# Loading each attention head's tiles half a head ahead, and parking three heads' outputs in DRAM

## The chip, the cores and the metric

The kernel runs on one core of one Trainium2 chip. The metric is the device time of one execution in microseconds (us). TensorE (PE) does the matrix products, VectorE (DVE), ScalarE (ACT) and GpSimd (POOL) the element-wise work, and SyncE (SP) issues nearly all transfers (DMAs) between DRAM and the on-chip memory SBUF; products are summed up in PSUM. SP issues its DMAs in the order of its program, and an issue that must wait holds all that stand behind it.

## The reference, cut to what matters

One layer on x of 1024 rows by 1024 columns in float32: half a feed-forward block, a mixer with two branches of attention, half a second feed-forward block, and a norm. The change lies in the mixer alone.

```
u = rms_norm(x, mix_norm)
q_a, k_a, v_a, q_b, k_b, v_b, gate_logits = split(u @ w_mix_in)
y_a = chunked_band_attention(q_a, k_a, v_a, rel_bias_a)     # branch A: 8 heads of 64
y_b = diff_attention(q_b, k_b, v_b, t5_bias, lam, subln_g)  # branch B: 4 heads of 128
g_a, g_b = split(sigmoid(gate_logits + b_gate))
merged = g_a * (y_a @ w_branch_a) + g_b * (y_b @ w_branch_b)
x = x + merged @ w_o
```

In branch A a chunk of 64 rows attends to itself and to the 8 chunks before it. In branch B each head has two score matrices; with a bias b the softmax of the second, times lam, is taken from the softmax of the first, and the difference is multiplied by v:

```
sc = einsum('bqhrd,bkhrd->bhrqk', qblk, k) * scale + bias   # r = 0, 1; keys up to the query's chunk
p = softmax(sc)
attn = p[:, :, 0] - lam * p[:, :, 1]
o = rms_norm(attn @ v, subln_g) * (1 - lambda_init)
```

## The kernel before, in words

All values of matrix products are kept as two parts, a rounded high part and the low rest, and a product takes three matmuls (high x high, high x low, low x high; `mm3`, lines L128 to L130).

The stage that changes lies between the mixer's projections, which write q, k, v and the gates g to DRAM, and the output projection. It has eight heads in a row: A0 to A3 (each of them two heads of branch A side by side) and B0 to B3. For a head `load_qkv` fetches four tiles of 1 MB: qs, ks, kl (k with its two parts swapped) and vt. They come from a pool `big` of 14 buffers of 1 MB, which also holds the bias tiles nb and the outputs y of the heads (1 MB each, high and low part of 1024 rows). A new tile takes the buffer of one that is done with; a load into it has to wait until the last reader of that one is through. nb is made by `bias_rows` with eight small DMAs from a table in DRAM; each A head has its own, B0 and B1 share one, B2 and B3 another. The outputs y of all eight heads stay in SBUF until they are multiplied by w_branch_a or w_branch_b.

Every head is cut into eight jobs. A job is a Python generator with five steps: scores (`sc`, L779, L780), bias and softmax (DVE at L787, ACT at L789); nothing; transposes of the probabilities (`pt`, L795); the product with vt (`pv`, L943, L944 in branch B); and in branch B the norm and a matmul that turns and scales the result (`try`, L958), whose split into high and low part is y (DVE at L104). `run` takes up a new job in each round and carries the four before it one step on, so that five jobs overlap, over the edges of heads as well. A head's first job issues the head's loads, in its own first step.

Beside the jobs of branch B runs a filler, `branch_a`: 16 steps, one for every two jobs of B. A step loads a gate tile gl (128 x 512), makes y_a @ w_branch_a for it (`pb`, 12 matmuls), multiplies by gl on DVE (L892) and stores the result ta (L893). `pb` takes a PSUM buffer of the tag "pv", which has two. After the stage the same is done with y_b and w_branch_b, where the gate and ta are loaded, and the results merged.

Each engine's order is settled when the kernel is built: a scheduler takes the instructions of all this and puts them in the order in which, by its own model of costs, they get ready. So a program text that issues a load earlier also moves other instructions against each other.

## Time and profile before

| | us |
|---|---|
| three runs of the kernel before | 2159.69, 2159.53, 2156.72 (median 2159.53) |
| the profiled execution, its own time | 2157.48 |
| its span in the trace | 2155.1 |
| PE busy | 2074.9 (96%) |
| DVE busy | 1460.8 (68%) |
| ACT busy | 975.0 (45%) |
| POOL busy | 193.3 (9%) |

The attention stage takes from about 1060 to 1355 us of the span; head B0's first scores stand at about 1175 and those of B3, the last head, at about 1293. In a profile's row the first column is the start in us, the second the time busy; x8 at its end says that eight like it stand together, and [1.41 <-DMA kl<-kx] that the engine stood idle for 1.41 us before, until that DMA had landed. "PEclk" is the granted clock of TensorE as a share of the higher of its two levels, 2.4 GHz.

### The profile page before, as it was taken

What the parts mean: (1) busy time and instruction counts of PE and PEld (TensorE: products, weight loads), DVE (VectorE), ACT (ScalarE), POOL (GpSimd) and SP (SyncE); (2) the same over time, 40 slices, a digit from 0 to 9 for tenths busy, and PEclk for the clock granted to TensorE, in tenths of its full rate; (3) what the DMA queues carried; (4) which work ended last, traced back from release to release, by engine and by line L of the source; (5) the groups of instructions that cost most, each with busy time, mean ns of one, the idle gap of its engine ahead of it and who ended that gap; (6) DMA issues with size and microseconds to landing.
All of it is one profiled execution on the core that took longest, in us unless ns stands there. A gap on an engine that the chain in (4) does not pass through costs nothing.

```text
span 2155.1 us, 29016 instructions
## 1 busy us (share of the span) xinstructions
PE 2074.9 (96%) x10025; PEld 1730.3 (80%) x10025; DVE 1460.8 (68%) x2678; ACT 975.0 (45%) x1911; POOL 193.3 (9%) x290
## 2 busy tenths in 40 slices
PE   6999999999999999999999988898999999999997
PEld 5788888888888788899788877776788888888886
DVE  7666566577577756566488877777766656658566
ACT  5433333334446544444498665135433333334444
POOL 2120000000001000000066233201000000000001
PEclk9999999999999999999999999999999999999999
DMA  6653333294345544553682365614643333366344
GB/s 193 174 169 111 96 95 118 93 336 133 118 130 158 169 143 164 195 196 137 224 279 103 134 210 184 230 59 157 181 156 92 114 94 96 114 244 220 98 118 156
DMA packets 277572, 333.55 MB, mean 155 GB/s; under 512 B 15421, under 2 KB 168013, under 8 KB 277425
## 3 DMA queue, kind: packets, MB, share of 16 engines
q1 hardware_dynamic: 276096, 327.94, 46.8%
q0 software_dynamic: 1184, 3.24, 0.6%
q8 instruction: 79, 1.29, 0.3%
q14 instruction: 69, 0.56, 0.1%
q10 hardware_dynamic: 144, 0.52, 0.1%
HBM read 226.45 MB, written 105.19 MB: 154 GB/s over the span
## 4 chain that ended last, share of the span: by engine, by line
PE 80%; DVE 7%; DMA 5%; ACT 4%; issue 3%; SPq 1%; POOL 0%; ACTq 0%; DVEq 0%; POOLq 0%
PE prod L128 19%; PE prod L129 19%; PE prod L130 18%; PE po L129 6%; PE po L130 6%; PE po L128 6%; DVE wlo L102 2%; ACT whi L97 1%; ACT pm L789 1%; PE tr L205 1%; PE pb L128 1%; PE pb L130 1%; PE pb L129 1%; PE pt L795 1%; PE sc L779 1%
## 5 line engine op out<-in xcount | busy, mean ns | idle before, releaser
L129 PE MATMUL po<-wlo,whi 128*128 128x512 f32 x728 | 285.2, 392 | 5.5 <-DVE wlo L102 5.4
L130 PE MATMUL po<-whi,wlo 128*128 128x512 f32 x728 | 283.9, 390 | 0.0
L97 ACT CAST whi<-raw 128x512 fp32r<-128x512 f32 x200 | 124.4, 622 | 311.5 <-PE prod L129 244.4
L97 ACT CAST whi<-T 128x512 fp32r<-128x512 f32 x196 | 121.9, 622 | 249.7 <-PE prod L129 228.5
L97 ACT CAST whi<-B 128x512 fp32r<-128x512 f32 x178 | 110.8, 623 | 266.1 <-PE po L129 258.2
L113 DVE TENSOR_TENSOR c<-prod,c 128x512 f32<-128x512 f32 x190 | 131.1, 690 | 133.3 <-PE prod L130 122.3
L102 DVE TENSOR_TENSOR wlo<-raw,whi 128x512 fp32r<-128x512 f32 x200 | 138.6, 693 | 106.2 <-ACT whi L97 64.8
L102 DVE TENSOR_TENSOR wlo<-B,whi 128x512 fp32r<-128x512 f32 x178 | 122.4, 688 | 127.3 <-ACT whi L97 127.3
L128 PE MATMUL po<-whi 128*128 128x512 f32 x728 | 198.8, 391 | 0.4 <-DVE xc L507 0.3
L102 DVE TENSOR_TENSOR wlo<-T,whi 128x512 fp32r<-128x512 f32 x196 | 134.6, 687 | 92.5 <-ACT whi L97 91.6
L139 POOL TENSOR_TENSOR r<-v,neg_half 128x1 f32<-128x1 f32 x64 | 50.3, 790 | 1324.2 <-DVE v L180 1225.9
L129 PEld LDWEIGHTS po<-wlo,whi 128*128 128x128 f32 x728 | 136.9, 188 | 38.0 <-DVE wlo L102 9.8
L128 PEld LDWEIGHTS po<-whi 128*128 128x128 f32 x728 | 136.7, 189 | 29.9 <-ACT whi L97 1.4
L130 PEld LDWEIGHTS po<-whi,wlo 128*128 128x128 f32 x728 | 136.9, 188 | 28.2
L102 DVE TENSOR_TENSOR wlo<-N,whi 128x512 fp32r<-128x512 f32 x64 | 44.1, 689 | 113.2 <-PE prod L129 62.9
L102 DVE TENSOR_TENSOR wlo<-ha,whi 128x512 fp32r<-128x512 f32 x154 | 105.4, 684 | 9.0 <-ACT whi L97 9.0
L272 ACT COPY c<-prod 128x512 f32<-128x512 f32 x186 | 103.1, 586 | 11.2 <-DMA hA<-c 4.3
L97 ACT CAST whi<-ha 128x512 fp32r<-128x512 f32 x154 | 94.8, 615 | 16.9 <-PE prod L129 11.4
L789 ACT ACTIVATE pm<-pm,mn 128x640 f32<-128x640 f32 (+7 forms) x128 | 94.0, 736 | 11.9 <-DVE ri L924 6.3
L128 PE MATMUL prod<-A11h,whi 128*128 128x512 f32 x240 | 95.7, 399 | 2.6 <-ACT A11h L97 2.6
L128 PE MATMUL prod<-S1h,whi 128*128 128x512 f32 x240 | 94.1, 392 | 3.1 <-ACT S1h L97 2.1
L787 DVE CUSTOM_DVE_ANT_0 pm<-sc,nb 128x640 f32<-128x640 f32 (+7 forms) x128 | 87.9, 698 | 12.5 <-PE sc L780 5.9
(246 smaller groups left out, 5369.4 us busy)
## 6 DMA issues: line engine op xcount, KB each, us to landing
raw<-in_ffn_w_in_dram SPq DMA_DIRECT2D x98, 512.0 KB, 4.4
raw<-in_w_mix_in_dram SPq DMA_DIRECT2D x47, 512.0 KB, 4.5
ha<-hS SPq DMA_DIRECT2D x88, 256.0 KB, 2.7
hA<-c SPq DMA_DIRECT2D x66, 256.0 KB, 4.3
ha<-hA SPq DMA_DIRECT2D x66, 256.0 KB, 2.7
B<-in_ffn_w_out_dram SPq DMA_DIRECT2D x12, 1024.0 KB, 10.3
hS<-hs SPq DMA_DIRECT2D x44, 256.0 KB, 3.0
hS<-c SPq DMA_DIRECT2D x44, 256.0 KB, 4.5
```

The source lines that it names most:

```text
L97: nc.scalar.copy(out=hi, in_=src)
L102: (nc.gpsimd if on_pool else nc.vector).tensor_tensor(out=lo, in0=src, in1=h, op=ALU.subtract)
L113: nc.vector.tensor_tensor(out=out_, in0=a, in1=b, op=op)
L128: nc.tensor.matmul(ps, a[0], b[0], start=first, stop=False, skip_group_check=shared)
L129: nc.tensor.matmul(ps, a[0], b[1], start=False, stop=False, skip_group_check=shared)
L130: nc.tensor.matmul(ps, a[1], b[0], start=False, stop=last, skip_group_check=shared)
L139: nc.gpsimd.tensor_tensor(out=r, in0=v, in1=neg_half, op=ALU.pow)
L205: nc.tensor.transpose(tr[:, k, :], rows[:, k * P:(k + 1) * P], ident)
L272: nc.scalar.copy(out=self.held[name], in_=p)
L779: nc.tensor.matmul(sc[:, m, :wc], qs[:, h, c], ks[:, h, kc], start=True, stop=False)
L787: nc.vector.tensor_tensor_reduce(out=d3, in0=sc, in1=nb.rearrange("p (n w) -> p n w", n=n), scale=1.0, scalar=3e38, op0=ALU.add, op1=ALU.m ...
L789: nc.scalar.activation(out=dst, in_=dst, func=AF.Exp, bias=mn, scale=-1.0, accum_out=rs)
```

## The change

A head's loads and its nb move from its first job into a function `begin`, which is put into the list of jobs by itself, behind the fourth job of the head before; `run` calls it there. The first head begins at once, and its qs, ks and kl are loaded in two halves (`load_qkv(pr, 2)`). y is still allocated in the first job. The last job of B0, B1 and B2 now stores the head's y to a new DRAM tensor `y_d`; behind the sixth job of B3 three calls of `load_y` take new tiles from the pool and load them back, and they, with B3's y from SBUF, are what the stage behind multiplies by w_branch_b.

```diff
@@ -572,6 +572,7 @@
     v_d = drams(2, [S, 2 * HALF], "v", F32R)
     g_d = drams(2 * KT, [P, S], "g")
     ta_d = drams(KT, [P, S], "ta")
+    y_d = drams(3, [P, 2, S], "y", F32R)
     diag_a = dram.tile([A_HEADS, SKEW, EA], F32, name="diag_a")
     diag_b = dram.tile([B_HEADS, SKEW, EB], F32, name="diag_b")
     rows = lambda a: [a[t * P:(t + 1) * P, :] for t in range(NT)]
@@ -746,7 +747,7 @@
         flush()
 
 
-    ys = []
+    ys, last_y = [], []
     with tc.tile_pool(name="ps2", bufs=1, space=PSUM) as ps:
         e1, e2 = (small.tile([P, 1], F32, tag="le", bufs=2, name="le") for _ in range(2))
         nc.scalar.activation(out=e1, in_=lams[0], func=AF.Exp)
@@ -808,9 +809,12 @@
 
 
 
-        def run(jobs, filler=None):
+        def run(jobs):
             live = []
-            for step, job in enumerate(list(jobs) + [None] * 4):
+            for job in list(jobs) + [None] * 4:
+                if callable(job):
+                    job()
+                    continue
                 for g in [job] + live[::-1] if job else live[::-1]:
                     next(g, None)
                 live = (live + [job] if job else live)[-4:]
@@ -819,14 +823,16 @@
         def jobs_a(pr):
             ctx_ = {}
 
+            def begin():
+                ctx_["qkv"] = load_qkv(pr, 1 if pr else 2)
+                ctx_["nb"] = big([P, 2, S], "nb", F32)
+                for hh in range(2):
+                    bias_rows(ctx_["nb"][:, hh, :WA], diag_a, 2 * pr + hh, EA, WA)
+
             def job(sb_, h):
-                if not ctx_:
-                    ctx_["qkv"] = load_qkv(pr)
+                if "y" not in ctx_:
                     ctx_["y"] = big([P, 2, S], "y")
                     ys.append(ctx_["y"])
-                    ctx_["nb"] = big([P, 2, S], "nb", F32)
-                    for hh in range(2):
-                        bias_rows(ctx_["nb"][:, hh, :WA], diag_a, 2 * pr + hh, EA, WA)
                 qkv, y, nb = (ctx_[n] for n in ("qkv", "y", "nb"))
                 vt = qkv[3]
                 i0, i1 = 2 * sb_, 2 * sb_ + 1
@@ -875,7 +881,7 @@
                 if h == 1:
                     c = slice(sb_ * 256, (sb_ + 1) * 256)
                     split(ysum, y[:, 0, c], y[:, 1, c], on_pool=True)
-            return [job(sb_, h) for sb_ in range(4) for h in range(2)]
+            return begin, [job(sb_, h) for sb_ in range(4) for h in range(2)]
 
 
         def branch_a():
@@ -897,16 +903,19 @@
         def jobs_b(hb, filler):
             ctx_ = {}
 
+            def begin():
+                ctx_["qkv"] = load_qkv(4 + hb)
+                if hb % 2 == 0:
+                    nbs.append(big([P, 2, S], "nb", F32))
+                    for hh in range(2):
+                        bias_rows(nbs[-1][:, hh, :], diag_b, hb + hh, EB, WB)
+                ctx_["nb"] = nbs[-1][:, hb % 2, :]
+
             def job(i):
-                if not ctx_:
-                    ctx_["qkv"] = load_qkv(4 + hb)
+                if "y" not in ctx_:
                     ctx_["y"] = big([P, 2, S], "y")
-                    ys.append(ctx_["y"])
-                    if hb % 2 == 0:
-                        nbs.append(big([P, 2, S], "nb", F32))
-                        for hh in range(2):
-                            bias_rows(nbs[-1][:, hh, :], diag_b, hb + hh, EB, WB)
-                    ctx_["nb"] = nbs[-1][:, hb % 2, :]
+                    if hb == 3:
+                        last_y.append(ctx_["y"])
                 qkv, y, nb = (ctx_[n] for n in ("qkv", "y", "nb"))
                 vt = qkv[3]
                 w = (i + 1) * P
@@ -958,18 +967,27 @@
                 nc.tensor.matmul(tr[:, 0, :], o1, dg, start=True, stop=True)
                 c = slice(i * P, (i + 1) * P)
                 split(tr[:, 0, :], y[:, 0, c], y[:, 1, c], scale=gsub)
-            return [job(i) for i in range(NT)]
-
-        jobs, nbs = [], []
-        for pr in range(4):
-            jobs += jobs_a(pr)
+                if i == NT - 1 and hb < 3:
+                    move(nc.sync, y_d[hb], y)
+            return begin, [job(i) for i in range(NT)]
+
+        def load_y(hb):
+            ys.append(big([P, 2, S], "y"))
+            move(nc.sync, ys[-1], y_d[hb])
+
+        nbs = []
         filler = branch_a()
         due = [0]
-        for hb in range(4):
-            jobs += jobs_b(hb, filler)
+        heads = [jobs_a(pr) for pr in range(4)] + [jobs_b(hb, filler) for hb in range(4)]
+        jobs = [heads[0][0]]
+        for n, (_, js) in enumerate(heads):
+
+            jobs += js[:4] + ([heads[n + 1][0]] if n < 7 else []) + js[4:6]
+            jobs += [lambda hb=hb: load_y(hb) for hb in range(3) if n == 7] + js[6:]
         run(jobs)
         for _ in filler:
             pass
+        ys.extend(last_y)
 
 
     with tc.tile_pool(name="ps3", bufs=1, space=PSUM) as ps:
```

The orders below are those of SP. qs, ks, kl and vt of B1 read q_180, k_188, kx_196 and v_200, those of B2 read q_181 and so on up by one, but v_200 for all heads of branch B; g_201 to g_208 are the gates of the filler, ta_217 to ta_224 its results, and of each of these a row has one half.

The first place is SP at head B0, before:

```order
L805 DMA nb<-diag_b 32x1024 x2
L119 DMA gl<-g_201 128x512
L893 DMA ta_217<-gl 128x512
L119 DMA gl<-g_201 128x512
L119 DMA wa<-in_w_branch_a_dram 128x4x256
L124 DMA qs<-q_180 128x2x1024
L124 DMA ks<-k_188 128x2x1024
L124 DMA kl<-kx_196 128x2x1024
L124 DMA vt<-v_200 128x8x256
```

The same place after, where nb is B0's:

```order
L806 DMA nb<-diag_b 32x1024 x2
L124 DMA qs<-q_180 128x2x1024
L124 DMA ks<-k_188 128x2x1024
L124 DMA kl<-kx_196 128x2x1024
L124 DMA vt<-v_200 128x8x256
L119 DMA gl<-g_201 128x512
L899 DMA ta_217<-gl 128x512
L119 DMA gl<-g_201 128x512
L124 DMA qs<-q_181 128x2x1024
L124 DMA ks<-k_189 128x2x1024
```

The four tiles of B1 stand ahead of the filler's first step, and those of B2 where those of B1 stood.

The second place is SP around the gate of g_203, before:

```order
L119 DMA gl<-g_203 128x512
L893 DMA ta_219<-gl 128x512
L124 DMA qs<-q_181 128x2x1024
L124 DMA ks<-k_189 128x2x1024
L124 DMA kl<-kx_197 128x2x1024
L119 DMA gl<-g_203 128x512
L124 DMA vt<-v_200 128x8x256
L805 DMA nb<-diag_b 32x960 x2
```

The same gate after; y_225 is B0's y in DRAM:

```order
L899 DMA ta_218<-gl 128x512
L124 DMA vt<-v_200 128x8x256
L119 DMA gl<-g_203 128x512
L806 DMA nb<-diag_b 32x960 x2
L899 DMA ta_219<-gl 128x512
L806 DMA nb<-diag_b 32x1024 x2
L806 DMA nb<-diag_b 32x960 x2
L124 DMA y_225<-y 128x2048
L806 DMA nb<-diag_b 32x1024 x2
L119 DMA gl<-g_203 128x512
```

vt of B2 stands ahead of the gate's first half, and the bias of B2 and B3 and the store of B0's output lie between the halves.

The third place is SP in the last head, before; raw is w_branch_b:

```order
L893 DMA ta_223<-gl 128x512
L119 DMA gl<-g_207 128x512
L119 DMA raw<-in_w_branch_b_dram 128x4x256 x2
L893 DMA ta_223<-gl 128x512
L119 DMA raw<-in_w_branch_b_dram 128x4x256 x2
L444 DMA B_14124<-in_w_o_dram 128x2x512
L119 DMA gl<-g_208 128x512
```

The same place after, with y_225, y_226 and y_227 for the outputs of B0, B1 and B2:

```order
L899 DMA ta_223<-gl 128x512
L124 DMA y_227<-y 128x2048
L119 DMA raw<-in_w_branch_b_dram 128x4x256
L124 DMA y<-y_225 128x2048
L124 DMA y<-y_226 128x2048
L124 DMA y<-y_227 128x2048
L119 DMA gl<-g_207 128x512
L119 DMA raw<-in_w_branch_b_dram 128x4x256 x3
L444 DMA B_14139<-in_w_o_dram 128x2x512
L119 DMA gl<-g_208 128x512
```

The last store of an output, and the loads of all three, stand between the gate's first half and its second.

## Rows read from the trace of the kernel before

**Rows 1.** The page's first lines: the span, PE's busy time with its count of instructions, and the shares of the chain that ended last by engine.

```profile
core 0 of [0], span 2155.1 us
...
PE 2074.9 (96%) x10025; PEld 1730.3 (80%) x10025; DVE 1460.8 (68%) x2678; ACT 975.0 (45%) x1911; POOL 193.3 (9%) x290
...
PE 80%; DVE 7%; DMA 5%; ACT 4%; issue 3%; SPq 1%; POOL 0%; ACTq 0%; DVEq 0%; POOLq 0%
```

**Rows 2.** The table of windows in the stage of branch A: start and end, length, busy time of PE, PEld, DVE, ACT and POOL with their instructions, granted clock, busy share of the DMA engines, GB/s.

```profile
1100.00:1125.00 25.00, 23.13 (x170) 20.76 (x167) 22.97 (x73) 23.33 (x61) 18.36 (x24) 1.00 0.77 271
1125.00:1150.00 25.00, 23.35 (x173) 21.31 (x173) 22.51 (x73) 22.58 (x59) 17.26 (x24) 1.00 0.39 127
1150.00:1175.00 25.00, 23.14 (x171) 20.83 (x169) 22.71 (x72) 22.79 (x60) 17.47 (x23) 1.00 0.48 162
```

**Rows 3.** PE's timeline: the first score matmuls of A2 and, two heads on, of B0.

```profile
1122.48 0.44 PE L779 MATMUL sc<-ks,qs 128*128 128x128 f32 x2
...
1175.53 0.39 PE L779 MATMUL sc<-ks,qs 128*128 128x128 f32 x2
```

**Rows 4.** The table of windows in branch B, with the columns of rows 2.

```profile
1196.00:1212.00 16.00, 13.59 (x80) 11.71 (x79) 14.13 (x40) 11.58 (x28) 4.00 (x8) 0.97 0.90 326
1212.00:1240.00 28.00, 27.09 (x161) 24.37 (x160) 24.39 (x78) 15.84 (x44) 8.52 (x17) 0.95 0.21 59
1240.00:1260.00 20.00, 15.76 (x94) 13.07 (x93) 13.90 (x45) 12.84 (x36) 7.70 (x14) 0.91 0.97 313
1260.00:1280.00 20.00, 19.47 (x118) 17.27 (x118) 17.43 (x55) 11.96 (x33) 6.11 (x12) 1.00 0.20 68
1280.00:1300.00 20.00, 16.03 (x104) 13.66 (x102) 16.11 (x52) 13.51 (x37) 6.69 (x12) 1.00 0.81 287
1300.00:1325.00 25.00, 24.51 (x150) 21.35 (x148) 21.81 (x69) 14.87 (x40) 8.69 (x17) 1.00 0.17 57
1325.00:1355.00 30.00, 19.81 (x128) 16.48 (x125) 17.08 (x49) 14.74 (x38) 10.69 (x20) 0.99 0.86 282
```

**Rows 5.** The timelines of PE and, in the fourth row, of DVE around the changes to heads B1, B2 and B3.

```profile
1209.94 0.44 PE L780 MATMUL sc<-kl,qs 128*128 128x128 f32 x2 [1.41 <-DMA kl<-kx]
...
1250.04 0.63 PE L130 MATMUL pb<-y,wlo 128*128 128x512 f32 x1
...
1252.61 0.39 PE L128 MATMUL pb<-y,whi 128*128 128x512 f32 x1
...
1256.70 0.29 DVE L787 CUSTOM_DVE_ANT_0 pm<-sc,nb 128x128 f32<-128x128 f32 x1 [1.46 <-DMA nb<-diag_b]
...
1257.06 0.38 PE L779 MATMUL sc<-ks,qs 128*128 128x256 f32 x1 [1.21 <-DVE mn L787]
...
1293.59 0.41 PE L779 MATMUL sc<-ks,qs 128*128 128x128 f32 x2 [2.17 <-DMA ks<-k]
```

**Rows 6.** SP's timeline: the second column is the time from the first issue's start to the last one's end.

```profile
1197.30 0.46 SPq L124 DMA_DIRECT2D qs<-q  x1
...
1199.74 5.57 SPq L893 DMA_DIRECT2D ta<-gl  x1
...
1237.24 0.43 SPq L124 DMA_DIRECT2D qs<-q  x1
...
1240.56 14.51 SPq L805 DMA_DIRECT2D nb<-diag_b  x8
...
1283.02 0.42 SPq L124 DMA_DIRECT2D qs<-q  x1
```

**Rows 7.** The view of the DMAs from 1190 to 1360: SP's queue with packets, MB and its share of 16 engines, and issues with their count, KB each and median us from issue to landing.

```profile
q1 hardware_dynamic: 17145, 30.96, 53.9%
...
gl<-g SPq DMA_DIRECT2D x19, 256.0 KB, 4.5
...
qs<-q SPq DMA_DIRECT2D x3, 1024.0 KB, 6.8
ks<-k SPq DMA_DIRECT2D x3, 1024.0 KB, 8.9
kl<-kx SPq DMA_DIRECT2D x3, 1024.0 KB, 11.6
vt<-v SPq DMA_DIRECT2D x3, 1024.0 KB, 14.4
```

**Rows 8.** The view of the tile nb from 1150 to 1360: its loads' time to landing.

```profile
DMA to landing us min/median/max: 2.6/3.6/14.5
```

**Rows 9.** The timelines of DVE (two rows) and PE (three) in the last head.

```profile
1338.01 0.69 DVE L892 TENSOR_TENSOR gl<-pb,gl 128x512 f32<-128x512 f32 x1 [2.35 <-DMA gl<-g]
...
1347.64 0.69 DVE L892 TENSOR_TENSOR gl<-pb,gl 128x512 f32<-128x512 f32 x1 [2.60 <-DMA gl<-g]
...
1338.76 0.50 PE L128 MATMUL pb<-y,whi 128*128 128x512 f32 x1 [1.64 <-DVE gl L892]
...
1353.90 0.49 PE L958 MATMUL try<-dg,o 128*128 128x128 f32 x2 [2.42 <-POOL dg L955]
1355.23 0.79 PE L128 MATMUL pb<-y,whi 128*128 128x512 f32 x1 [0.84 <-DVE y L104]
```

**Rows 10.** DVE's timeline: the last split of B2's y, and the reciprocal ahead of the multiply of 1338.01.

```profile
1320.64 0.34 DVE L104 SCALAR_TENSOR_TENSOR y<-try,gsub,y 128x128 fp32r<-128x128 f32 x1
...
1334.19 0.15 DVE L922 RECIPROCAL ri<-rs 128x1 f32<-128x1 f32 x1
```

## The prediction

> **What bounds the kernel now.** I read the page's header and its first part, then the chain of waits, then a table of windows over the attention stage, and last each engine's own rows where that table shows a hole. TensorE (PE) is busy 2074.9 of 2155.1 us, 96%, and 80% of the chain that ended last is PE [rows 1]. So only time in which PE stands still, or runs at a lower clock, can be won. The change touches 1060 to 1355 us. In the stage of branch A (1100 to 1175) PE is busy 23.1 to 23.4 us of each 25, and ACT and DVE just as much; heads follow one another every 26.5 us, with no wait for a load before a head's first score matmul [rows 2, 3]. In branch B the undisturbed stretches (1212 to 1240, 1260 to 1280, 1300 to 1325) hold 27.09 + 19.47 + 24.51 = 71.07 us of PE in 73: PE is the bound there, 2.6% idle. Between them lie the three changes of head, with 13.59 of 16, 15.76 of 20 and 16.03 of 20, and the last head's end with 19.81 of 30 [rows 4].
>
> At the head changes the trace names the cause: PE waits 1.41 us for kl (head B1) and 2.17 for ks (B3); at B2 DVE waits 1.46 for the bias tile nb and PE 1.21 for DVE after it [rows 5]. The loads were issued only at 1197.30, 1237.24 and 1283.02 [rows 6], just as the head began, and four loads of 1 MB together land after 6.8, 8.9, 11.6 and 14.4 us, some 2.5 us for each further MB [rows 7].
>
> **The loads half a head ahead.** Work on PE, DVE, ACT and POOL stays the same; what goes is waiting.
> - Idle time: the three windows hold 2.41 + 4.24 + 3.97 = 10.62 us without PE. At the 2.6% of the undisturbed stretches their 56 us would hold 1.5. Gain 9.1.
> - Clock: the granted clock is 0.97, 0.95 and 0.91 in 1196 to 1212, 1212 to 1240 and 1240 to 1260 [rows 4], behind holes in PE's work; a matmul of 512 columns takes 0.63 at 1250.04 and 0.39 at 1252.61, which is the higher level again [rows 5]. As lost time: 0.03 x 16 + 0.05 x 28 + 0.09 x 20 = 3.7. Without the holes I take all of it as won. Sum 12.8.
> - Branch A: no load is waited for now, so nothing is won; what the changed order moves I take as 0, with 3 us either way: PE's idle time there is 1.65 to 1.87 of 25 [rows 2].
> - First head in two parts: two halves of three tiles are three more DMAs on SP, 0.4 us each as the issues of [rows 6], beside PE's last products of the stage before. 0.
>
> What is late next? B1's tiles are now issued in the middle of B0 and are long there. B2's qs, ks and kl come right behind B0's last score (their buffers are B0's). The bias tile of B2 and B3 takes the buffer of B1's q, so it can be issued only behind B1's last score: it still comes late, but nothing large is ahead of it now, and its pieces land after 3.6 us in the median (2.6 at least, 14.5 at most) [rows 8]. DVE gets to it after about that time; I take 0, and 1.46 (what it waits now) as the other end.
>
> One new wait is plain in SP's order. vt of B2 stands ahead of gl of g_203, and vt of B3 ahead of gl of g_205. vt's buffer is free only after the last pv of the head two before, and SP issues in order: eight nb issues hold SP for 14.51 us from 1240.56 on [rows 6]. Behind vt wait the gl load, the gate multiply on DVE (L892, L898 after) and then PE, for the product's PSUM buffer is one of two that pv shares. The nearest rows are the gate's two waits for gl now, 2.35 and 2.60 us on DVE, of which PE shows 1.64 at 1338.76 [rows 9]. I take 1.0 on PE for each of two, 2.0; the ends are 0 and 2 x 2.60 = 5.2.
>
> **The three outputs through DRAM.** 3 MB are stored and 3 MB loaded. At 2.5 us for each MB of queue that is 15 us, in 155 us (1200 to 1355) whose queue of SP is busy 53.9% [rows 7]: it is hidden, if the places are right. The first two stores lie within heads B2 and B3, whose windows 1260 to 1280 and 1300 to 1325 use 0.20 and 0.17 of the DMA engines [rows 4]. The third is another matter. y_227's store waits for DVE's last y of head B2 (T0, 1320.64 us now [rows 10]); behind it on SP stand a raw load, the three loads of y and then gl of g_207, second half. The load of y_227 waits for that store's landing, and so does gl behind it.
>
> T0 to gl: the raw load waits for a buffer that PE frees some 4 us after T0. y_225 and y_226 are ready. y_227 was issued just after T0; a single MB lands in about 5 us by the rows (gl, 256 KB, takes 4.5 and the first of four MB 6.8 [rows 7]). The loads thus start at T0 + 4, the first lands 6.8 later, each further one 2.5 later; gl, at their end, lands at about T0 + 4 + 6.8 + 2 x 2.5 + 1 = T0 + 17. (The Trainium skill, "DMA: Bandwidth & Descriptors", section "Two DMAs through the same engine are not ordered", has it that a DMA which reads what an earlier one wrote must have the issuing engine wait on the first one's semaphore, and that the same queue doesn't stand in for it. That speaks against the change: SP stands still at y_227's load. No run here shows this pair yet; the nearest in the trace, ta stored and loaded as tA, lies far apart. Its section "Anatomy of one DMA — SWDGE (gpsimd) path" gives 2.0 us and bytes over 436 GB/s; my estimate from that for 1 MB is 4.4, which would make T0 + 17 no later.)
>
> DVE gets to that multiply after three splits of y and the reciprocals behind them, in the order now at 1334.19, T0 + 13.4 [rows 10]. It would then wait some 4 us, where the tail has 2.35 + 2.60 of such waits now, at two other multiplies [rows 9]. One of these may become shorter, since everything behind shifts with it. Three multiplies now lie behind T0 that need gl late (two before). I take +2 us for the tail. Lower end -5.0, both waits of today gone; upper end +8, a wait of 17 + 5 - 13.4 = 8.6 with nothing given back. PE's other waits in the tail (2.42 for POOL's dg at 1353.90 [rows 9]) are the work's own length at the end and stay.
>
> **Sum.** -9.1 - 3.7 + 2.0 + 2.0 = -8.8 us. The profiled execution took 2157.48 (span 2155.1 and 2.38 around it), so 2148.7. The runs' median 2159.53 lies 2.05 above the profiled one: 2150.7, say 2151. What a measurement of this kernel can tell from no change is about 0.2%, 4.3 us.
>
> **The rivals.**
> - The tail's waits go too. SP issues the ta stores and gl loads late because each waits for work ahead; with the new order gl could be there in time. For it: the tail has 10.2 us without PE [rows 4]. Against: three more MB land just there. -12.8 + 2.0 - 5.0 = -15.8, 2144.
> - SP's order takes most of it back. Upper ends of both waits for vt (5.2) and a tail of +4: -12.8 + 5.2 + 4 = -3.6, 2156. For it: SP's queue already has rows of 5.57 and 14.51 us [rows 6].
> - It doesn't do what it says at one change of head: nb still gates B2. That window keeps its 4.24 - 0.53 idle and 1.8 of clock, 5.5 in all: -8.8 + 5.5 = -3.3, 2156. For it: nb's buffer isn't free any earlier. Against: in the window of today 4 MB are ahead of it.
> - Slower: the way of head B2's output through DRAM becomes the end of the last head. Store 14.4 us (the last of the four MB of a load, [rows 7]), load 6.8 to 14.4 behind it, gl 4.5: T0 + 25.7 to T0 + 33.3, against 13.4, so DVE waits 12.3 to 19.9 at the multiply and PE follows; the clock that falls behind such a hole costs another 1.8, as after 1250. In place of +2 that is +14 to +22: net +3.4 to +10.9, 2163 to 2170. It decides once the tail grows by over 10.8 us. For it: the store can't start before T0, and B3 has only 34.3 us left from there to the first product of the next stage at 1355.23 [rows 9, 10]. Against: little else is moved at T0 (share 0.17 [rows 4]).
>
> **How the numbers follow.** Forecast (-5 to -13) 0.42; tail gains too 0.16; SP's order 0.20; nb 0.08; the way through DRAM 0.14. The first two are faster by more than 4.3 us, and of the third and fourth, which lie at -3.6 and -3.3, about a fifth: 0.64. The rest of those two is within 0.2%: 0.22. The last is slower: 0.14. The range goes from 2142, just under the second case, to 2163, where the slower case begins; outside are most of the slower case and a little below, under 0.2.
>
> **What would show it.** Right: at the changes to B1, B2 and B3 no PE row waits for kl or ks, PE is idle under 1 us in each of these windows, and the clock is 0.99 or more in 1212 to 1260. The vt term: a wait of DVE at L898 for gl of about 2 us, in the first half of heads B1 and B2. The tail: y_227's load issued some 5 us after its store, gl behind it, and one wait at L898 of about 4 us. Wrong: SP standing over 10 us between y_227's store and its load, or the stage from the last score of B0 to the first product of the next stage as long as before though the head changes have closed; then something else than the loads set the pace in branch B.

## The result and the profile after

The changed kernel takes 2161.64 us (median of 20 runs), the kernel before 2157.77 (20 runs): a ratio of 1.0016, 95% interval [1.0009, 1.0022], so 0.16% or 3.5 us slower. Forecast were 2151 and 8.8 us faster; the range held the time, the direction was wrong. One execution says less here than the runs: the same order of the attention stage took 279.05 us in one profile and 282.13 in another kernel's (e1 below). So verdicts below go by the ratios, and the profiles say where.

The page of the changed kernel, its first lines, which answer to [rows 1]:

```profile
core 0 of [0], span 2158.2 us
...
PE 2077.1 (96%) x10025; PEld 1730.0 (80%) x10025; DVE 1463.7 (68%) x2678; ACT 976.5 (45%) x1911; POOL 197.6 (9%) x290
...
PE 81%; DVE 6%; DMA 6%; ACT 3%; issue 2%; SPq 1%; POOL 0%; DVEq 0%; ACTq 0%; POOLq 0%
```

Next, the table of windows cut at four places of the program, with the columns of [rows 2]: the attention stage from its first score to the first product with w_branch_b, from there to the first transposes of the second feed-forward block, and the start of that block up to its first S2 product (the rest, some 596 us in both, is left out). First the kernel before:

```profile
1076.94:1355.23 278.29, 247.64 (x1601) 216.75 (x1601) 230.43 (x720) 200.07 (x529) 129.84 (x193) 0.99 0.55 185
1355.23:1493.00 137.77, 129.73 (x553) 103.97 (x553) 107.78 (x170) 48.67 (x92) 17.07 (x13) 0.97 0.42 141
1493.00:1558.40 65.40, 61.16 (x292) 48.79 (x292) 50.22 (x83) 34.33 (x62) 3.24 (x5) 0.95 0.61 184
```

and the changed one:

```profile
1075.73:1354.78 279.05, 248.94 (x1601) 215.55 (x1601) 233.13 (x720) 201.14 (x529) 132.15 (x189) 0.99 0.60 205
1354.78:1490.69 135.91, 128.41 (x552) 102.42 (x552) 107.68 (x170) 48.63 (x93) 17.05 (x13) 0.98 0.44 148
1490.69:1561.98 71.29, 64.42 (x293) 51.67 (x293) 50.69 (x83) 34.68 (x62) 3.16 (x5) 0.89 0.56 169
```

Two things are to be seen. The attention stage has won nothing: 30.1 us without PE (279.05 - 248.94), 30.7 before. And a stretch that the diff doesn't touch, the start of the second feed-forward block, is 5.9 us longer, at a granted clock of 0.89 (0.95 before).

Branch B of the changed kernel in the windows of [rows 4]:

```profile
1196.00:1212.00 16.00, 14.88 (x89) 12.53 (x87) 14.12 (x42) 11.55 (x28) 5.57 (x11) 1.00 0.79 296
1212.00:1240.00 28.00, 25.64 (x161) 22.62 (x161) 23.49 (x74) 17.53 (x50) 10.81 (x20) 1.00 0.26 85
1240.00:1260.00 20.00, 17.11 (x106) 14.52 (x106) 17.44 (x58) 13.98 (x40) 8.63 (x13) 1.00 0.97 338
1260.00:1280.00 20.00, 18.20 (x114) 16.22 (x112) 15.36 (x48) 11.43 (x30) 5.76 (x12) 1.00 0.28 97
1280.00:1300.00 20.00, 17.38 (x96) 14.29 (x97) 17.25 (x58) 13.57 (x36) 7.69 (x12) 1.00 0.48 158
1300.00:1325.00 25.00, 22.76 (x147) 20.31 (x145) 21.78 (x65) 15.22 (x41) 7.34 (x14) 1.00 0.23 84
```

The heads begin some 4 to 10 us earlier here, so single windows correspond only roughly. The three at the changes of head hold 6.63 us without PE (10.62 before), and the clock is 1.00 in all six rows, as the prediction wanted it. But the three that were undisturbed now hold 6.40 (1.93 before). Together that is 13.03 us against 12.55: the holes have become smaller, and as much idle time has come up between them.

Did the waits for loads go? They did, and others stand in their place. Groups of PE's instructions by line in the whole stage (count, busy time, mean ns, idle time before them and who ended it); the kernel before:

```profile
L779 PE MATMUL sc<-ks,qs 128*128 128x320 f32 (+4 forms) x192 | 66.9, 358 | 6.7 <-DVE mn L787 3.1 <-DMA ks<-k 2.2 <-ACT sig L721 0.8
L780 PE MATMUL sc<-kl,qs 128*128 128x320 f32 (+4 forms) x192 | 61.7, 331 | 1.4 <-DMA kl<-kx 1.4
```

and the changed one:

```profile
L780 PE MATMUL sc<-ks,qs 128*128 128x320 f32 (+4 forms) x192 | 68.3, 361 | 9.5 <-DVE mn L788 7.6 <-ACT sig L722 0.8
L781 PE MATMUL sc<-kl,qs 128*128 128x320 f32 (+4 forms) x192 | 62.1, 328 | 0.0
```

The 3.6 us for ks and kl [rows 5] are gone, while the scores' wait for DVE's softmax (mn) grew from 3.1 to 7.6: no tile is late, but PE now comes to scores whose buffer DVE hasn't emptied yet. That this belongs to the order, and not to the earlier loads, other runs show: with the loads just as early, but the engines in the order of the kernel before, that wait is 2.1 us (e3 below) and 1.9 (e12).

The timeline of the last head, SP's rows and under them DVE's multiply, which answer to [rows 9, 10]:

```profile
1320.08 0.32 SPq L124 DMA_DIRECT2D y<-y  x1
...
1323.35 1.45 SPq L124 DMA_DIRECT2D y<-y  x3
1324.90 0.38 SPq L119 DMA_DIRECT2D gl<-g  x1
...
1337.00 0.69 DVE L898 TENSOR_TENSOR gl<-pb,gl 128x512 f32<-128x512 f32 x1 [2.98 <-DMA gl<-g]
```

The store of B2's output is issued at 1320.08 and all three loads by 1324.80. The one that needs the store, the last of the three, thus went out at most 4.7 us behind it. The view of the DMAs issued from 1320.0 to 1320.4, with the store's time to landing at its end, and SP's wait for that store (us in total, times, longest) in another kernel with the same store and loads (e13 below):

```profile
y<-y SPq DMA_DIRECT2D x1, 1024.0 KB, 3.9
...
SPq L125 <- DMA y<-y: 0.7, 1, 0.7
```

(The Trainium skill, "DMA: Bandwidth & Descriptors", section "Two DMAs through the same engine are not ordered", wants the issuing engine to wait for the store before it issues such a load. In the changed kernel no wait is seen, for the store had landed before the load's turn came; in e13 SP stands still for it, 0.7 us.) The landings, 3.9 us here and 4.8 in e13, lie on either side of the estimate of 4.4 in the prediction. The gate behind the loads makes DVE wait 2.98 us, where 4 were forecast.

### The profile page after: what moved, and what is told of

Its sections match the earlier page's. It is cut to its first block, busy times and chain, and to the rows that moved or that the text cites. A ratio compares the mean times of both kernels' runs of the same rounds, so it can differ in the third digit from the quotient of the medians.

```text
span 2158.2 us, 29047 instructions
## 1 busy us (share of the span) xinstructions
PE 2077.1 (96%) x10025; PEld 1730.0 (80%) x10025; DVE 1463.7 (68%) x2678; ACT 976.5 (45%) x1911; POOL 197.6 (9%) x290
## 4 chain that ended last, share of the span: by engine, by line
PE 81%; DVE 6%; DMA 6%; ACT 3%; issue 2%; SPq 1%; POOL 0%; DVEq 0%; ACTq 0%; POOLq 0%
PE prod L128 19%; PE prod L129 18%; PE prod L130 18%; PE po L129 6%; PE po L130 6%; PE po L128 6%; DVE wlo L102 2%; DMA ha<-hS 1%; DMA raw<-in_ffn_w_in_dram 1%; PE tr L205 1%; DMA gl<-g 1%; PE sc L780 1%; ACT whi L97 1%; PE pt L796 1%; PE pb L128 1%
## 5 line engine op out<-in xcount | busy, mean ns | idle before, releaser
L139 POOL TENSOR_TENSOR r<-v,neg_half 128x1 f32<-128x1 f32 x64 | 55.1, 865 | 1307.9 <-DVE v L180 1228.3
```

Source lines behind the costliest of these rows:

```text
L139: nc.gpsimd.tensor_tensor(out=r, in0=v, in1=neg_half, op=ALU.pow)
```

## The experiments

In several of them an order is held fixed: behind the traced program stands a table of places, and each instruction of an engine gets an edge to the one that is to stand ahead of it, so that the scheduler keeps that order and is free with the rest (SP above all: its order follows from that of the others, and differs with it).

```
+ for eng, (lo, deltas) in ORDER.items():
...
+     for x, y in zip(want, want[1:]):
+         tc.add_manual_dep(y, x.name, mb.DependencyInfo(mb.DependencyClass.NoSync, mb.DependencyReason.DATA),
+                           reason="keep_order")
```

A ratio is against the kernel before on the same chip; 0.1% is 2.2 us. "This order" of a kernel means that of PE, DVE, ACT and POOL.

| kernel | median us | ratio, 95% interval |
|---|---|---|
| changed | 2161.64 | 1.0016 [1.0009, 1.0022] |
| e1 changed, order behind the stage as before | 2158.23 | 1.0003 [0.9995, 1.0012] |
| e2 before, order behind the stage as changed | 2160.67 | 1.0019 [1.0009, 1.0028] |
| e3 changed, order of before everywhere | 2171.96 | 1.0067 [1.0055, 1.0079] |
| e4 as e3, gates on ACT | 2164.34 | 1.0033 [1.0021, 1.0045] |
| e5 as e1, gates on ACT | 2160.64 | 1.0013 [0.9999, 1.0026] |
| e6 before, gates on ACT | 2156.55 | 0.9991 [0.9981, 1.0] |
| e7 outputs through DRAM alone, order of before | 2170.25 | 1.0056 [1.0039, 1.0073] |
| e8 before without the loads of B1 to B3 | 2152.09 | 0.9975 [0.9964, 0.9986] |
| e9 as e1, nothing through DRAM | 2160.81 | 1.0019 [1.001, 1.0029] |
| e10 loads ahead alone, order of before | 2169.91 | 1.0064 [1.0049, 1.0079] |
| e11 as e9, gates on ACT | 2158.62 | 1.0006 [0.9994, 1.0017] |
| e12 as e10, gates ahead of tiles | 2154.66 | 0.9982 [0.9973, 0.9991] |
| e13 as e3, gates ahead of tiles | 2162.33 | 1.002 [1.0008, 1.0032] |
| e14 as e1, gates ahead of tiles | 2158.79 | 1.0006 [0.9995, 1.0017] |
| e15 as e13, outputs behind a gate | 2163.08 | 1.0024 [1.0015, 1.0033] |

**e1 and e2: the order behind the stage.** The edit is the table alone, 229 places on PE, 50 on DVE, 40 on ACT, 3 on POOL.

> The changed kernel, with only the order of PE, DVE, ACT and POOL between the output projection and the second feed-forward block's first products set back to that of the kernel before (229 places on PE, 50 on DVE); the attention stage as changed. Theory O (the scheduler's new order there costs the time): that stretch goes from 71.3 us back to about 65.4, and the run to about 2161.6 - 5.9 = 2156. Rival S (it is the state in which the engines arrive: earlier by 2.3 us, with other tiles in flight or a lower clock): the stretch stays at 70 or more, the run at 2160 to 2162.

> The kernel before, with only that order of the stretch behind the attention stage taken from the changed kernel. Theory O: the stretch goes from 65.4 to about 71, the run to about 2157.8 + 5.9 = 2163.5. Rival S: no change, 2157 to 2159.

The third window of e1:

```profile
1493.04:1558.65 65.61, 61.17 (x292) 48.68 (x293) 50.25 (x83) 34.38 (x62) 2.88 (x5) 0.95 0.62 184
```

and of e2:

```profile
1491.76:1560.67 68.91, 62.25 (x293) 49.70 (x293) 50.63 (x83) 34.72 (x62) 2.88 (x5) 0.93 0.58 175
```

With the old order the stretch is back at 65.6, and with the new one put into the kernel before it goes to 68.9: theory O holds, and rival S falls as the whole cause (e2 brings back 3.5 of the 5.9 us; whether the rest is the state in which the engines arrive, or chance between executions, stays open). PE's timeline shows the place, a wait for DVE's S1l (the low part of a value of that block) that neither the kernel before nor e1 has; first the changed kernel, then e2:

```profile
1532.45 1.11 PE L205 MATMUL tr<-ident,xt 128*128 128x128 f32 x4 [4.07 <-DVE S1l L102]
...
1530.94 0.66 PE L205 MATMUL tr<-ident,xt 128*128 128x128 f32 x4 [2.22 <-DVE S1l L102]
```

By the runs the order behind the stage is worth 0.13% (changed against e1) and 0.19% (e2), some 3 to 4 us, less than the 5.9 that one profile showed. With the old order there the changed kernel is no slower than before (1.0003). So the loss that was measured arises behind the stage; the times expected under theory O, 2156 and 2163.5, were both some 2 to 3 us too far out.

**e3: only transfers moved.** The table takes the order of the kernel before everywhere.

> The changed kernel (loads half a head ahead, three outputs through DRAM), with the order of PE, DVE, ACT and POOL of the kernel before everywhere, so that only transfers are moved. Theory O applied to the attention stage too (loads were the cause of the holes, and the scheduler's new order gave the gain away): the stage goes from 279.1 to about 278.3 - 9 = 269, the run to about 2148. Rival P (the holes at the changes of head belong to the chain of DVE, ACT and POOL in the short jobs, and the loads only stood in the same place): the stage stays within 2 us of 278, the run at 2155 to 2158.

Both missed: 14 us slower. The view of the tile gl (idle time of DVE ahead of it, and in how many places):

```profile
  DMA gl<-g: 20.4, 8
```

DVE waited for gates 20.4 us, 5.6 in the kernel before. The timeline of one of them, SP's rows and DVE's:

```profile
1207.53 0.37 SPq L124 DMA_DIRECT2D qs<-q  x1
1208.00 0.42 SPq L124 DMA_DIRECT2D ks<-k  x1
1208.47 0.46 SPq L124 DMA_DIRECT2D kl<-kx  x1
1208.98 0.79 SPq L119 DMA_DIRECT2D gl<-g  x1
...
1218.73 0.69 DVE L898 TENSOR_TENSOR gl<-pb,gl 128x512 f32<-128x512 f32 x1 [3.86 <-DMA gl<-g]
```

A gate issued behind 3 MB of tiles comes ten us later; the 4.5 of [rows 7] is the median. PE waits 14.2 us in all for such gate multiplies. The forecast had priced this waiting at 2.0, and only behind vt. And the new order in the stage (the scheduler's, with the SP order that comes with it), which is what differs between e3 and e1, is worth 0.64%, 14 us: it doesn't give the gain away, it hides the cost.

That a gate comes late behind tiles wasn't new. In the kernel before one stands behind B2's qs, ks and kl as well; the view of the DMAs issued from 1238.7 to 1239.5, with the time to landing at its end, and DVE's multiply with that gate:

```profile
gl<-g SPq DMA_DIRECT2D x1, 256.0 KB, 11.0
...
1251.22 0.67 DVE L892 TENSOR_TENSOR gl<-pb,gl 128x512 f32<-128x512 f32 x1
```

It was issued at 1238.83 and took 11.0 us, but its multiply came only 12.4 us after the issue, and nothing waited. In e3 DVE is ready for the gate 5.9 us after its issue (1218.73 - 3.86 - 1208.98).

**e4 to e6: the gates on another queue.**

```
- gl = load(g_d[j][:, c], temp([P, HALF], "gl"))
+ gl = temp([P, HALF], "gl")
+ nc.scalar.dma_start(out=gl, in_=g_d[j][:, c])
```

> As the run before it (loads half a head ahead, outputs through DRAM, the order of PE, DVE, ACT and POOL of the kernel before everywhere), but the 16 gate loads gl of the filler are issued by ACT, so that no load of vt or y stands ahead of them on a queue. Theory G (early loads do close the holes, but SP's order makes the gates late: DVE waited 20.4 us for gl in that run): PE's waits for DVE's gate multiply go from 14.2 us to under 3, the stage from 294 to 278.3 - 4 to 9 = 269 to 274, the run to 2148 to 2153. Rival P (the holes at the changes of head belong to the short jobs' chain): the waits for gl go, but the stage stays at 278 or more, the run at 2157 or more.

> The changed kernel with the order behind the attention stage of the kernel before (as the first run), and the gates' loads issued by ACT; the scheduler may order the attention stage as it likes. Theory G: DVE's waits for gl (5.7 us) go, and with them 2 to 4 us, the run at 2153 to 2156. Rival P: as the first run, 2157 to 2159.

> The kernel before with the gates' loads issued by ACT: the control of the two runs above. Both theories: its waits for gl (5.6 us on DVE, 2.2 on PE) go, those for kl, ks and nb stay: 2154 to 2157.

e4 wins 0.34% on e3. Its time lies where rival P has it, but it decides nothing between the two, for the waits that both let go have stayed: DVE still waits 14.6 us for gates. The timeline, ACT's row and DVE's:

```profile
1208.73 0.33 ACTq L895 DMA_DIRECT2D gl<-g  x1
...
1215.75 0.69 DVE L899 TENSOR_TENSOR gl<-pb,gl 128x512 f32<-128x512 f32 x1 [2.42 <-DMA gl<-g]
```

On a queue of its own the gate takes 7.0 us, for the tiles that SP issued at 1206 to 1207 are still under way: another queue removes SP's order, not the competition for the transfers. (The quickest of the gates on ACT's queue lands in 2.5 us.) e5 is no better than e1 (theory G missed by 5 us), the control e6 at the edge of measuring. In both the waits for gates, which were to go, grew: to 10.3 us on DVE in e5 (6.2 in e1) and to 6.9 in e6 (5.6 in the kernel before). So what e6 wins, if anything, isn't the gates' waiting.

**e7: the outputs through DRAM alone.** Loads stand at each head's first job again.

```
- jobs += js[:4] + ([heads[n + 1][0]] if n < 7 else []) + js[4:6]
+ jobs += [begin] + js[:6]
...
```

> The three outputs go through DRAM as in the changed kernel, but each head's loads stand at its own first job, and PE, DVE, ACT and POOL have the order of the kernel before. The forecast's own step: the stores and the first two loads cost nothing, and the load of the third makes the gate behind it late by some 4 us: +2, bounds -5 to +8, so 2152 to 2165, likeliest 2159. Theory G: of the 14.2 us in which PE waited for the gate multiply in the run with early loads and this order, the last wait of 6.17 us belongs to the outputs and shows here too: 2162 to 2164.

12 us slower, above the forecast's bound of +8 and above theory G's 2162 to 2164: both missed. The timeline, SP's rows and PE's at the change to B2, and DVE's in the last head:

```profile
1240.86 0.32 SPq L124 DMA_DIRECT2D y<-y  x1
1241.23 0.43 SPq L124 DMA_DIRECT2D qs<-q  x1
...
1251.34 0.66 PE L780 MATMUL sc<-ks,qs 128*128 128x128 f32 x2 [3.72 <-DMA ks<-k]
...
1351.42 0.69 DVE L898 TENSOR_TENSOR gl<-pb,gl 128x512 f32<-128x512 f32 x1 [7.05 <-DMA gl<-g]
```

The output's store waits for the head's end and holds the next head's loads behind it, so that PE waits 3.72 us for ks where it waited for nothing of that tile before. In the last head DVE waits 7.05 us for a gate behind the outputs.

**e8: no loads at the changes of head.** Heads B1 to B3 compute on B0's tiles: their own q, k and v are left out.

```
- ctx_["qkv"] = load_qkv(4 + hb)
+ ctx_["qkv"] = b_tiles[0] if b_tiles else load_qkv(4)
+ b_tiles.append(ctx_["qkv"])
...
```

> The kernel before with its own order of PE, DVE, ACT and POOL, and no loads of qs, ks, kl and vt for heads B1, B2 and B3: these compute on B0's tiles (the output leaves those heads' own q, k, v out), so nothing at the changes of head can wait for a tile. This bounds what any earlier load can win with that order. The forecast's step (the holes and the slow clock behind them are the loads'): the stage goes from 278.3 to about 265.5, the run to 2145. Theory H (most of the holes are the chain of DVE, ACT and POOL in the short jobs; only the waits that name a load, 1.41 + 1.21 + 2.17 = 4.8 us, can go): the stage at 272 to 276, the run at 2152 to 2156.

The windows of the three changes of head, which answer to those of [rows 4]:

```profile
1196.00:1212.00 16.00, 14.53 (x88) 12.40 (x86) 15.37 (x43) 11.69 (x30) 5.25 (x8) 1.00 0.21 67
...
1240.00:1260.00 20.00, 18.18 (x106) 15.70 (x107) 16.56 (x58) 14.72 (x43) 9.54 (x15) 0.91 0.35 105
...
1280.00:1300.00 20.00, 17.09 (x104) 14.21 (x104) 16.90 (x57) 14.17 (x41) 8.13 (x14) 1.00 0.22 78
```

With nothing to load 6.2 us of these 56 are still without PE (10.6 before), and the clock is still 0.91 at B2. PE's waits there name DVE, POOL and ACT alone, and none over 0.9 us. The whole gain is 0.25%, 5.4 us: theory H holds, and the forecast's 12.8 is out of reach in that order.

**e9 to e11: loads ahead, nothing through DRAM.**

```
- if hb == 3:
-     last_y.append(ctx_["y"])
+ ys.append(ctx_["y"])
...
- if i == NT - 1 and hb < 3:
-     move(nc.sync, y_d[hb], y)
...
```

> The changed kernel without the way through DRAM (all eight outputs stay in SBUF; loads stand half a head ahead, and wait where no buffer is free, as two tiles of B3 do), with the order behind the attention stage of the kernel before. Against the first run (the same with the way through DRAM, 2158). Theory R (the way through DRAM costs several us in the changed order as well): 2152 to 2155. Theory H: 2157 to 2159, the way through DRAM is hidden there.

> As the run before it (ahead, nothing through DRAM), but PE, DVE, ACT and POOL in the order of the kernel before everywhere. The costs so far in that order: both parts +14.8, the way through DRAM alone +12. If they add up (theory H): about +3, 2160. The forecast's step (-12.8 from the loads, given back by the outputs): 2146 to 2150.

> The ahead-only kernel (order behind the stage as before) with the gates' loads issued by ACT: a version that might beat both kernels. If the gain of the control with gates on ACT (-2) adds to it: 2 us under the ahead-only run; 2150 to 2156.

e9 missed both: without the outputs it is no faster than e1. In its SP order kl and vt of B3, which find no buffer sooner, stand ahead of the two gates of g_205, and DVE waits 8.3 us for gates (6.2 in e1); that this is the whole cause wasn't tried. e10 shows that costs don't add up either: 14 us for the loads alone, 12 for the outputs alone, 14 for both. The timeline of e10, SP's rows and DVE's:

```profile
1289.43 0.37 SPq L124 DMA_DIRECT2D vt<-v  x1
1289.89 0.53 SPq L119 DMA_DIRECT2D gl<-g  x1
...
1298.08 0.69 DVE L898 TENSOR_TENSOR gl<-pb,gl 128x512 f32<-128x512 f32 x1 [6.29 <-DMA gl<-g]
```

This is the new wait that the forecast named, a gate behind vt of B3. It takes 6.29 us on DVE and 6.12 on PE behind it, where I had 1.0 on PE, with 2.60 as the end. e11 gains on e9 what e6 gains on before, about 0.1%, and ends where before is; and as there, DVE's waits for gates are longer with the gates on ACT (12.9 us against 8.3).

**e12 to e14: the gates ahead of the tiles.** On SP five loads of B2 and B3 get an edge to the gate load that had stood behind them; the edit holds nothing else over e10, e3 and e1.

```
+ GATES_FIRST = [((6, 0), 2), ((6, "vt"), 4), ((7, 0), 5), ((7, 2), 8), ((7, "vt"), 9)]
...
+ for tile, gate in GATES_FIRST:
+     tc.add_manual_dep(tiles[tile].ins, gates[gate].ins.name,
+                       mybir.DependencyInfo(mybir.DependencyClass.NoSync, mybir.DependencyReason.DATA),
+                       reason="gates_first")
```

> The ahead-only kernel in the order of the kernel before (e10), with one thing more: on SP five tile loads of heads B2 and B3 stand behind the gate load of the filler that stood behind them before. Theory G (early loads cost time because gates stand behind tiles on SP and in the transfers; 18.2 us of DVE's waits and 13.5 of PE's there): DVE's waits for gl fall to 6 or less, the stage from 292.5 to 272 to 276, what the kernel without those loads took (272.6), and the run to 2151 to 2155, faster than both kernels. Rival Q (what is dear is the traffic itself, wherever it stands, or the order): the waits move elsewhere and the stage stays above 280, the run above 2160.

> Both parts of the change in the order of the kernel before (e3), with the same five loads behind the gates. Theory G: the waits of heads B1 and B2 go (some 8 us of e3's 14.2 on PE), that at the end of 6.17 us, behind the three outputs, stays: the run goes from 2172 to about 2160 to 2164. Rival Q: 2168 or more.

> The changed kernel with the order behind the stage of the kernel before (e1, 2158) and the same five loads behind the gates; the scheduler orders the attention stage anew. Theory G: DVE's waits for gl (6.2 us) fall, the run at 2154 to 2157. Rival Q: no change, 2157 to 2160.

The view of gl in e12:

```profile
  DMA gl<-g: 4.9, 3
```

and its windows at the changes of head:

```profile
1196.00:1212.00 16.00, 14.90 (x88) 12.76 (x87) 15.40 (x45) 11.84 (x28) 5.34 (x10) 1.00 0.36 113
...
1240.00:1260.00 20.00, 18.04 (x100) 15.32 (x100) 15.53 (x50) 14.26 (x40) 8.59 (x13) 0.83 0.57 197
...
1280.00:1300.00 20.00, 17.39 (x100) 14.38 (x99) 15.63 (x52) 13.19 (x37) 7.71 (x13) 0.91 0.40 132
```

18.2 us of DVE's waits for gates fall to 4.9, and the run from 1.0064 to 0.9982, 15 us by five edges (2169.91 - 2154.66). PE's busy time in the windows is that of the kernel without loads, within 0.4 us, though at a lower clock (0.83 and 0.91 in the last two, against 0.91 and 1.00) and with 10 matmuls fewer. Theory G holds for the loads, and e12 is faster than both kernels, by 3.9 us [1.9, 5.8] against before. e13 came as theory G has it: of e3's cost two thirds go, and 8 us remain over e12. e14 didn't: 6.1 us of waits for gates remain in the order that the scheduler chose for it, and the time is that of e1, as rival Q has it. So the five edges pay in the old order only.

**e15: what remains of the outputs.** The three loads get an edge to the first gate load of g_208.

```
- GATES_FIRST = [..., ((7, "vt"), 9)]
+ GATES_FIRST = [..., ((7, "vt"), 9), ((8, 0), 14), ((8, 1), 14), ((8, 2), 14)]
```

> As e13 (both parts, order of the kernel before, tiles behind gates), but the three loads of outputs stand on SP behind the first gate load of the last step's pair (g_208), not ahead of it. Theory G (outputs cost as tiles did, by what stands behind them): DVE's wait of 6.96 us for that gate falls to about 2.4, as without outputs, the run from 2162 to 2156 to 2159. Rival Q (the traffic of 6 MB in the last heads costs it wherever the loads stand): the wait moves to the last gate or to the first products of the next stage, the run stays at 2160 to 2164.

The time is rival Q's. The last head's end in e12, from about the end of the last split of B2's y to the next stage:

```profile
1319.00:1354.00 35.00, 25.20 (x150) 21.04 (x148) 21.27 (x60) 16.91 (x44) 12.35 (x22) 0.94 0.75 250
```

in e13:

```profile
1319.89:1364.84 44.95, 29.55 (x151) 24.78 (x149) 21.34 (x59) 17.18 (x43) 12.30 (x22) 0.80 0.86 304
```

and in e15:

```profile
1320.80:1363.30 42.50, 27.45 (x150) 23.17 (x148) 21.41 (x59) 17.04 (x43) 12.28 (x22) 0.82 0.91 324
```

DVE's timeline there, in e13:

```profile
1343.57 0.69 DVE L901 TENSOR_TENSOR gl<-pb,gl 128x512 f32<-128x512 f32 x1 [6.96 <-DMA gl<-g]
```

and in e15:

```profile
1353.67 0.69 DVE L901 TENSOR_TENSOR gl<-pb,gl 128x512 f32<-128x512 f32 x1 [7.49 <-DMA gl<-g]
```

The wait of 6.96 us goes from one gate to the next, 7.49, and the run stays. Two causes can be seen. The share of the transfers in this stretch is 0.75 without the outputs and 0.86 to 0.91 with them, over a longer time, and 1.01, the whole, from 1338 to 1350 in e15; the granted clock falls from 0.94 to about 0.8 behind the hole. But the second gate of g_208 also still stands behind the outputs on SP. SP's largest wait from 1339 to 1349 in e15 (us in total, times, longest):

```profile
SPq L120 <- DMA y<-y: 3.8, 2, 2.5
```

SP, with loads of xc to issue first, waits for the outputs to land, so that the gate is issued only at 1348.37 (1343.24 in e12), and it takes 5.3 us to land (3.2). How much of the 8 us the traffic costs wherever it stands isn't settled: a place behind both gates wasn't tried.

## Why the prediction was wrong

The measured cost comes apart like this: both parts in the old order 1.0067 (e3), the new order in the stage -0.64% (e1 against e3), the new order behind it +0.13% (changed against e1): 1.0016. The forecast had terms for a part of the first of these three only; what the changed order moves it took as 0 in branch A, and for the rest it had no term. That the time still lies in its range is luck: neither the late gates, nor the order that hides most of them, nor the cost of the order behind the stage is what the range was made of.

- **"At the 2.6% of the undisturbed stretches their 56 us would hold 1.5. Gain 9.1", and 3.7 of clock.** The mechanism was right, the size wrong: 5.4 us at most (e8). In the changed kernel the clock came as forecast, 1.00 in all of 1196 to 1325, and no PE row waits for kl or ks; but the windows at the changes of head still hold 1.12, 2.89 and 2.62 us without PE where under 1 each was the sign, and the stretches between them lose what is won. I put all idle time at a change of head down to the loads, though the rows named a load, or nb, for 1.41 + 1.21 + 2.17 = 4.79 of 10.62. The rest is the chain of ACT, POOL and DVE behind short jobs with little for PE beside them; it stays when nothing is loaded, and so, in the old order, does a clock of 0.91.
- **"I take 1.0 on PE for each of two, 2.0."** The new wait was the right one and its place too, but in the old order it measured 6.29 on DVE and 6.12 on PE at one gate (e10), and the gates behind qs, ks and kl had no term at all. In the old order the early loads cost 0.89% over no loads (e10 against e8), and e12 takes back nearly all of it by five edges. The bound was taken from DVE's waits of today, not from the time to landing: a gate behind 3 MB took 11.0 us in the kernel before as well, only nothing waited for it.
- **"It is hidden, if the places are right", of the outputs' 6 MB.** Wrong: 12 us alone (e7), still 8 with the gates first (e13 against e12), and in e15 another place, behind one gate and ahead of the next, doesn't mend it. The 53.9% was a mean over heads; 4 of the 6 MB fall into a window whose share of the transfers stood in [rows 4] as 0.86.
- **The tail, "+2".** For the changed kernel nearly right: from B2's last split to the next stage 35.1 us (1319.70 to 1354.78) against 34.6, with the wait of 2.98 where 4 was forecast. But it isn't the forecast's sum that came true: the idle time in that stretch fell by 1.9 us, to 8.5, where it was to grow by 2, and PE's busy time grew by 2.4 (26.60 us from 1319.70 on, 24.17 before), with 156 matmuls against 152 at a granted clock of 0.93 against 0.99.
- **"Work on PE, DVE, ACT and POOL stays the same; what goes is waiting."** The work did, the order didn't, and this is the step that failed by most. In the stage the new order hides some 14 us of late gates and outputs and pays with 4.5 us more of the scores' wait for DVE. Behind it, where not a line was changed, it costs 3 to 4 us, and with that it decides the sign: without it the time is that of the kernel before (e1).
- Of the rivals "SP's order takes most of it back" was the nearest, but in the old order only: gates late behind tiles, all gain gone (e10). In the changed kernel as it ran, DVE waits 5.9 us for gates, 5.6 before. "The way through DRAM becomes the end of the last head" fell as I had put it: the store lands after 3.9 us, not 14.4. That nb gates B2 fell as well: in the changed kernel no wait for nb is seen there.
- Two readings in the prediction were off by little and change nothing: the reciprocal at 1334.19 stands 13.55 us behind T0, not 13.4, and from T0 to 1355.23 are 34.6 us, not 34.3.

## What to carry to other kernels

Of the idle time around a late load only about the part whose rows name that load can be won by loading earlier (here 4.8 us were named and 5.4 won); leaving the load out altogether, with the order held fixed, measures that ceiling in one run. A load that is moved ahead moves ahead of something: list what stands behind it on its queue, small urgent transfers above all, and let those go first (here five edges on SP were worth 15 us with the order of the engines held, and nothing in the order that the scheduler chose). For each, compare its time to landing with the moment at which it is needed; that nothing waits for it today says little about its bound. Where a scheduler sets the order, compare the orders of the whole program and hold the old one fixed in a second kernel, or the change is charged with what another order does somewhere else.

## What the runs showed of the hardware

A gate of 256 KB, 4.5 us in the median, takes ten us when it is issued just behind three tiles of 1 MB on the same queue (1208.98 to 1218.73 in e3; 11.0 us in the kernel before) and still 7.0 when it is issued on ACT's queue 1.8 us after them (e4, where the quickest takes 2.5): tiles on one queue slow down a load on the other. Sending the outputs through DRAM, 4 MB of it in a stretch whose transfers stand at 0.75 (e12), makes the run some 8 us longer, ahead of a gate (e13) or between two (e15). And identical instructions in another order, with the same loads, differ by 3 to 4 us in a run of 2158 (e1, e2).
